# A fused low-rank projection: the pipeline re-made with hand-placed semaphores, bf16 pairs turned as fp32 words

## The chip, the cores and the metric

The kernel runs on one core of a Trainium2 chip. The core has a matrix engine (PE, with a separate row PEld for its weight loads), a vector engine (DVE), an activation engine (ACT), a general-purpose engine (GpSimd, called POOL in the profile), and SyncE (SP), which here only issues transfers. Sixteen DMA engines move data between the chip's memory (HBM) and the on-chip memory (SBUF, 128 partitions). PE writes its results to PSUM[...]. The metric is device time in microseconds (us), median of the runs; lower is better.

## What is computed

```python
x_flat = x.reshape(-1, in_dim)          # 32768 x 256, fp32
y = x_flat @ W                          # W 256 x 256
lora_out = x_flat @ lora_A              # rank 16
lora_out = lora_out * lora_E
lora_out = lora_out @ lora_B
y = y + scale * lora_out                # 32768 x 256, fp32
```

All factors on the right are small, so the kernel first builds one 256 x 256 matrix, W + scale * (lora_A * lora_E) @ lora_B, and then does one product with x. x and y are 33.55 MB each and have to be read and written once.

## The kernel before

The 32768 rows are cut into 8 chunks of 4096 rows (4 MB). In a chunk each of the 128 partitions holds 32 whole rows, so that a chunk's load or store is one contiguous run of 32 KB per partition. There are six chunk buffers in SBUF, called homes; a chunk's result is written over its own input, and the store leaves from there. A program that plans waits and semaphores by itself (the tile framework) decides the waits between engines; each engine works in the order of the code.

All transfers are issued by SyncE on one queue, in the order written in the list ORDER (lines 19 to 22): loads of chunks 0 to 5, then stores S0 and S1, load 6, store 2, load 7, stores 3 to 7. Chunk 0 is loaded in three pieces (8, 8 and 16 rows per partition), and the four small inputs are loaded after the first piece (lines 77 to 84). Loads 6 and 7 reuse the homes of chunks 0 and 1, so they wait until those stores have landed. A store waits until the whole chunk is computed.

The set-up (lines 89 to 108) makes an identity matrix on GpSimd, turns lora_A with PE, scales it on DVE, multiplies with lora_B on PE, and adds W on DVE into weff, in bf16.

The main loop (lines 110 to 133) handles a chunk in 16 groups of CG = 2 rows per partition, 256 rows. [...] x is turned first: four fp32 transposes of 128x128 into PSUM (psum_xt, line 118), a cast to bf16 by ACT from PSUM to SBUF (xt, line 123), four bf16 matmuls of 256 columns into psum_y (line 126), and a copy by DVE into the home (line 133). psum_xt and psum_y have three buffers each, xt has six. There are 128 such groups.

Of the kernel before, what the change touches and what calls it, by code (L numbers as in the profile page):

```python
# [1 line left out]

# [5 lines left out]

P = 128
FP32 = mybir.dt.float32  # L10
BF16 = mybir.dt.bfloat16


ROWS = 32
N_CHUNKS = 8
N_HOMES = 6
LOAD_PIECES = {0: [8, 8, 16]}

ORDER = [
    "L0", "L1", "L2", "L3", "L4", "L5",  # L20
    "S0", "S1", "L6", "S2", "L7", "S3", "S4", "S5", "S6", "S7",
]
CG = 2


@with_exitstack
def kernel(
    ctx: ExitStack,
    tc: tile.TileContext,
    x: bass.AP,  # L30
    W: bass.AP,
    lora_A: bass.AP,
    lora_B: bass.AP,
    lora_E: bass.AP,
    scale: bass.AP,
    out: bass.AP,
):
    nc = tc.nc
    x_flat = x.flatten_outer_dims()
    out_flat = out.flatten_outer_dims()  # L40
    N, K = x_flat.shape
    M = out_flat.shape[1]
    R = lora_B.shape[0]
    KC = K // P
    assert N == N_CHUNKS * ROWS * P and K == M

    const = ctx.enter_context(tc.tile_pool(name="const", bufs=1))
    homes_pool = ctx.enter_context(tc.tile_pool(name="homes", bufs=1))
    xTpool = ctx.enter_context(tc.tile_pool(name="xTpool", bufs=6))
    ps_setup = ctx.enter_context(tc.tile_pool(name="ps_setup", bufs=1, space=bass.MemoryType.PSUM))  # L50
    ps_xT = ctx.enter_context(tc.tile_pool(name="ps_xT", bufs=3, space=bass.MemoryType.PSUM))
    ps_y = ctx.enter_context(tc.tile_pool(name="ps_y", bufs=3, space=bass.MemoryType.PSUM))

    x_chunks = x_flat.rearrange("(c p b) k -> c p b k", p=P, b=ROWS)
    y_chunks = out_flat.rearrange("(c p b) m -> c p b m", p=P, b=ROWS)

    homes = [
        homes_pool.tile([P, ROWS, K], FP32, name=f"home{h}", tag=f"home{h}")
        for h in range(N_HOMES)
    ]  # L60

    def load(c, s, e):
        nc.sync.dma_start(out=homes[c % N_HOMES][:, s:e, :], in_=x_chunks[c, :, s:e, :])  # L63

    def store(c, s, e):
        nc.sync.dma_start(out=y_chunks[c, :, s:e, :], in_=homes[c % N_HOMES][:, s:e, :])

    def pieces(c):
        s = 0
        for n in LOAD_PIECES.get(c, [ROWS]):  # L70
            yield s, s + n
            s += n

    first = list(pieces(0))
    load(0, *first[0])

    w_sb = const.tile([P, KC, M], FP32)
    nc.sync.dma_start(out=w_sb, in_=W.rearrange("(c p) m -> p c m", p=P))  # L78
    a_sb = const.tile([P, KC, R], FP32)
    nc.sync.dma_start(out=a_sb, in_=lora_A.rearrange("(c p) r -> p c r", p=P))  # L80
    e_sb = const.tile([R, 1], FP32)
    nc.sync.dma_start(out=e_sb, in_=lora_E[:, None])
    b_sb = const.tile([R, M], FP32)
    nc.sync.dma_start(out=b_sb, in_=lora_B)

    for s, e in first[1:]:
        load(0, s, e)

    ident = const.tile([P, P], FP32)
    make_identity(nc, ident)  # L90

    ps_at = ps_setup.tile([R, KC, P], FP32, name="ps_at")
    for c in range(KC):
        nc.tensor.transpose(ps_at[:, c, :], a_sb[:, c, :], ident)  # L94
    ate = const.tile([R, KC, P], FP32)
    nc.vector.tensor_scalar(
        out=ate,
        in0=ps_at,
        scalar1=e_sb,
        scalar2=float(scale),  # L100
        op0=mybir.AluOpType.mult,
        op1=mybir.AluOpType.mult,
    )
    ps_aeb = ps_setup.tile([P, KC, M], FP32, name="ps_aeb")
    for c in range(KC):
        nc.tensor.matmul(ps_aeb[:, c, :], ate[:, c, :], b_sb, start=True, stop=True)  # L106
    weff = const.tile([P, KC, M], BF16)
    nc.vector.tensor_add(out=weff, in0=w_sb, in1=ps_aeb)

    def compute(c):  # L110
        home = homes[c % N_HOMES]
        for g in range(ROWS // CG):
            psum_xt = ps_xT.tile([P, CG, KC, P], FP32, name="psum_xt")
            xt = xTpool.tile([P, CG, KC, P], BF16, name="xt")
            psum_y = ps_y.tile([P, CG, M], FP32, name="psum_y")
            for j in range(CG):
                for k in range(KC):
                    nc.tensor.transpose(  # L118
                        psum_xt[:, j, k, :],
                        home[:, g * CG + j, k * P:(k + 1) * P],  # L120
                        ident,
                    )
            nc.scalar.copy(out=xt, in_=psum_xt)  # L123
            for j in range(CG):
                for k in range(KC):
                    nc.tensor.matmul(  # L126
                        psum_y[:, j, :],
                        xt[:, j, k, :],
                        weff[:, k, :],
                        start=(k == 0),  # L130
                        stop=(k == KC - 1),
                    )
            nc.vector.tensor_copy(out=home[:, g * CG:(g + 1) * CG, :], in_=psum_y)  # L133

    done = -1
    for step in ORDER:
        c = int(step[1:])
        if step[0] == "L":
            if c:
                for s, e in pieces(c):  # L140
                    load(c, s, e)
        else:
            while done < c:
                done += 1
                compute(done)
            store(c, 0, ROWS)


# [1 line left out]
_INS = ['x', 'W', 'lora_A', 'lora_B', 'lora_E', 'scale']  # L150
_OUTS = [((16, 2048, 256), 'float32')]

_NUMBERS = {'scale': 1.0}


# [26 lines left out]
```

## Time and profile before

| what | value |
|---|---|
| time, median of 3 runs | 165.19 us (165.09 to 165.42) |
| span of the profiled run | 163.4 us |
| PE busy | 131.9 us (81%) |
| PE weight loads busy | 101.6 us (62%) |
| DVE busy | 83.8 us (51%) |
| ACT busy | 70.3 us (43%) |
| GpSimd busy | 0.7 us |
| DMA | 67.56 MB, mean 414 GB/s |

The span is the time from the first to the last instruction of the profiled run; the device time is a little longer. An engine's busy share is an average over the whole span, and says nothing on whether another engine waits for it. The page cuts the span into 40 slices of about 4.1 us, with one digit of busy share (in tenths) for each engine and for the DMA engines, so one can see which row is full where. The group lines give, for one line of code, the operation, its shape, how often it ran, its mean duration and what it waited for:

```profile
L123 ACT CAST xt<-psum_xt 128x512 bf16<-128x512 f32 x128 | 69.0, 588 | 73.5 <-PE psum_xt L118 73.4
L126 PE MATMUL psum_y<-weff,xt 128*128 128x256 bf16 x512 | 71.9, 279 | 6.5 <-ACT xt L123 2.2
L133 DVE COPY home_73<-psum_y 128x512 f32<-128x512 f32 x32 | 20.8, 686 | 15.3 <-PE psum_y L126 15.3
```

The first line reads: ACT ran 128 casts of 512 elements per partition, 69.0 us in all, 588 ns each, and stood idle 73.5 us before them, nearly all of it until PE had finished a transpose.

### The profile page before, as it was taken

Reading aid. Unit: us, or ns where it says so; the run is one execution under the profiler, and the core shown is the slowest. Engines: PE = TensorE matmul, PEld = TensorE weight load, DVE = VectorE, ACT = ScalarE, POOL = GpSimd, SP = SyncE. Lnnn points to the kernel's source line nnn. Section 1 sums busy time; section 2 is a strip of 40 time slices with the busy share of each in tenths; the row PEclk is TensorE's granted clock in tenths of the full one; section 3 lists DMA queues with packets and bytes.
Section 4 is the critical chain, followed back from the end, with each engine's and each line's share of the span. In section 5 each row is a group of like instructions: output and inputs, shape, how many; then the busy total and the mean of one; then the engine's idle time right before and its main releaser. Section 6 shows DMA issues by size and latency. Waiting matters only on the chain.

```text
span 163.4 us, 2576 instructions
## 1 busy us (share of the span) xinstructions
PE 131.9 (81%) x1030; PEld 101.6 (62%) x1030; DVE 83.8 (51%) x130; ACT 70.3 (43%) x129; POOL 0.7 (0%) x6
## 2 busy tenths in 40 slices
PE   0399998999999999999999999998999899940000
PEld 0278775777777777777777777767777677730000
DVE  0115666466666666666666666665566556650000
ACT  3022555455555555555555555554555555520000
POOL 1000000000000000000000000000000000000000
PEclk9999999999999999999999999999999999997555
DMA  5999999998999998999999999999999999999991
GB/s 191 393 447 453 409 489 381 457 441 385 477 417 387 473 413 377 443 441 405 457 409 425 469 393 441 449 397 433 451 393 469 409 433 465 393 437 449 393 425 64
DMA packets 3211, 67.56 MB, mean 414 GB/s; under 512 B 624, under 2 KB 896, under 8 KB 896
## 3 DMA queue, kind: packets, MB, share of 16 engines
q1 hardware_dynamic: 3200, 67.41, 96.9%
q8 instruction: 8, 0.13, 0.3%
q14 instruction: 3, 0.02, 0.0%
HBM read 33.85 MB, written 33.55 MB: 413 GB/s over the span
## 4 chain that ended last, share of the span: by engine, by line
PE 58%; ACT 22%; issue 5%; DMA 3%; ACTq 1%; SPq 0%; DVEq 0%; DVE 0%
PE psum_y L126 43%; ACT xt L123 22%; PE psum_xt L118 13%; DMA a_sb<-in_lora_A_dram 3%; PE ps_aeb L106 1%; ACTq L123 1%; DVEq L177 0%; PE ps_at L94 0%; SPq L78 0%; SPq L63 0%; DVE home_74 L133 0%
## 5 line engine op out<-in xcount | busy, mean ns | idle before, releaser
L123 ACT CAST xt<-psum_xt 128x512 bf16<-128x512 f32 x128 | 69.0, 588 | 73.5 <-PE psum_xt L118 73.4
L126 PE MATMUL psum_y<-weff,xt 128*128 128x256 bf16 x512 | 71.9, 279 | 6.5 <-ACT xt L123 2.2
L126 PEld LDWEIGHTS <-xt 128*128 128x128 bf16 x512 | 40.5, 99 | 34.5 <-ACT xt L123 31.0
L133 DVE COPY home_73<-psum_y 128x512 f32<-128x512 f32 x32 | 20.8, 686 | 15.3 <-PE psum_y L126 15.3
L133 DVE COPY home_74<-psum_y 128x512 f32<-128x512 f32 x32 | 20.6, 686 | 13.0 <-PE psum_y L126 13.0
L118 PE MATMUL psum_xt<-ident,home_73 128*128 128x128 f32 x128 | 19.1, 295 | 0.0
L118 PEld LDWEIGHTS psum_xt<-ident,home_73 128*128 128x128 f32 x128 | 16.4, 154 | 1.0 <-issue 0.7
L118 PE MATMUL psum_xt<-ident,home_74 128*128 128x128 f32 x128 | 16.6, 273 | 0.0
L118 PEld LDWEIGHTS psum_xt<-ident,home_74 128*128 128x128 f32 x128 | 14.5, 141 | 0.2
L133 DVE COPY home_75<-psum_y 128x512 f32<-128x512 f32 x16 | 10.3, 686 | 6.1 <-PE psum_y L126 6.1
L133 DVE COPY home_76<-psum_y 128x512 f32<-128x512 f32 x16 | 10.3, 686 | 6.1 <-PE psum_y L126 6.1
L133 DVE COPY home_77<-psum_y 128x512 f32<-128x512 f32 x16 | 10.3, 686 | 6.1 <-PE psum_y L126 6.1
L133 DVE COPY home_78<-psum_y 128x512 f32<-128x512 f32 x16 | 10.3, 686 | 6.1 <-PE psum_y L126 6.1
L118 PE MATMUL psum_xt<-ident,home_75 128*128 128x128 f32 x64 | 8.5, 273 | 0.0
L118 PE MATMUL psum_xt<-ident,home_76 128*128 128x128 f32 x64 | 8.5, 273 | 0.0
L118 PE MATMUL psum_xt<-ident,home_77 128*128 128x128 f32 x64 | 8.5, 273 | 0.0
L118 PE MATMUL psum_xt<-ident,home_78 128*128 128x128 f32 x64 | 8.5, 273 | 0.0
L118 PEld LDWEIGHTS psum_xt<-ident,home_76 128*128 128x128 f32 x64 | 7.3, 141 | 0.1
L118 PEld LDWEIGHTS psum_xt<-ident,home_78 128*128 128x128 f32 x64 | 7.3, 141 | 0.1
L118 PEld LDWEIGHTS psum_xt<-ident,home_75 128*128 128x128 f32 x64 | 7.3, 141 | 0.1
L118 PEld LDWEIGHTS psum_xt<-ident,home_77 128*128 128x128 f32 x64 | 7.3, 141 | 0.1
L94 PE MATMUL ps_at<-ident,a_sb 128*16 128x128 f32 x2 | 0.6, 394 | 6.8 <-DMA a_sb<-in_lora_A_dram 6.8
(12 smaller groups left out, 6.7 us busy)
## 6 DMA issues: line engine op xcount, KB each, us to landing
home_74<-in_x_dram SPq DMA_DIRECT2D x2, 4096.0 KB, 24.4
out_dram<-home_73 SPq DMA_DIRECT2D x2, 4096.0 KB, 33.9
out_dram<-home_74 SPq DMA_DIRECT2D x2, 4096.0 KB, 26.8
home_75<-in_x_dram SPq DMA_DIRECT2D x1, 4096.0 KB, 29.1
home_76<-in_x_dram SPq DMA_DIRECT2D x1, 4096.0 KB, 38.0
home_77<-in_x_dram SPq DMA_DIRECT2D x1, 4096.0 KB, 47.4
home_78<-in_x_dram SPq DMA_DIRECT2D x1, 4096.0 KB, 57.4
home_73<-in_x_dram SPq DMA_DIRECT2D x1, 4096.0 KB, 19.3
```

Source lines behind the costliest of these rows:

```text
L94: nc.tensor.transpose(ps_at[:, c, :], a_sb[:, c, :], ident)
L106: nc.tensor.matmul(ps_aeb[:, c, :], ate[:, c, :], b_sb, start=True, stop=True)
L118: nc.tensor.transpose(psum_xt[:, j, k, :], home[:, g * CG + j, k * P:(k + 1) * P], ident,)
L123: nc.scalar.copy(out=xt, in_=psum_xt)
L126: nc.tensor.matmul(psum_y[:, j, :], xt[:, j, k, :], weff[:, k, :], start=(k == 0), stop=(k == KC - 1),)
L133: nc.vector.tensor_copy(out=home[:, g * CG:(g + 1) * CG, :], in_=psum_y)
```

## The change

The planned waits are replaced by hand-placed semaphores in one block (a critical block in the framework's words), in which each engine has its own program. The computation of a group changes too:

- A group has CG = 4 rows per partition, 512 rows; there are 64 groups.
- GpSimd first casts the fp32 rows to bf16 into a staging buffer (stage, two buffers).
- PE turns the staged rows as fp32 words: one word holds a pair of neighbouring bf16 values, so one row of 256 values is 128 words and needs one 128x128 transpose in place of two. There are 256 transposes in place of 512.
- ACT copies the turned words from PSUM to SBUF and takes the even and odd halves apart (psum_xt read as bf16 with a step of two), since after the turn partition q holds the inputs 2q and 2q+1. The matrix weff is laid out to match: W and lora_A are loaded with "(q t) m -> q t m", which is one contiguous run per partition.
- The 8 matmuls of a group, 512 in all, are as before; DVE copies 1024 elements per partition at once.
- PE's program is a hardware loop of 10 rounds with 6 groups each, and 4 groups after it; it takes semaphores by waiting for 1 and counting down. The other engines' programs are written out.
- Buffers are fixed: two stage, two xt, two psum_xt and three psum_y[...].

Its purpose is to take work off PE and off the planner's synchronisation. SyncE's order of transfers, the six homes and the three first pieces stay. The core of the diff:

```diff
-CG = 2
+CG = 4
+GPC = ROWS // CG
+N_GROUPS = N_CHUNKS * GPC
+NS, NX, NT, NY = 2, 2, 2, 3
...
+    stage = [sbuf(f"stage{i}", [P, CG, K], BF16) for i in range(NS)]
+    xt = [sbuf(f"xt{i}", [P, CG, KT, P], BF16) for i in range(NX)]
...
+    with tc.tile_critical(no_gpsimd_drain=True):
+        with nc.Block(no_gpsimd_drain=True) as block:
+            @block.sync
+            def _(sync):
...
+                    if c >= N_HOMES:
+                        sync.wait_ge(stored_of[c - N_HOMES], 16)
+                    sync.dma_start(out=home[:, s:e, :], in_=x_chunks[c, :, s:e, :]).then_inc(loaded[pc], 16)
...
+                        sync.wait_ge(s_chunk, c + 1)
+                        sync.dma_start(out=y_chunks[c], in_=homes[c % N_HOMES][:]).then_inc(
+                            stored_of.get(c, stored_rest), 16
+                        )
+                sync.wait_ge(stored_rest, 16 * (N_CHUNKS - len(stored_of)))
...
+            @block.gpsimd
...
+                    if g >= NS:
+                        gpsimd.wait_ge(s_turned, g - NS + 1)
+                    gpsimd.tensor_copy(
+                        out=stage[g % NS][:], in_=homes[c % N_HOMES][:, b:b + CG, :]
+                    ).then_inc(s_stage, 1)
...
+                def turn(i):
+                    take(s_stage)
+                    words = stage[i % NS][:].bitcast(FP32)
+                    for b in range(CG):
+                        ins = tensor.transpose(psum_xt[i % NT][:, b, :], words[:, b, :], ident[:])
+                    ins.then_inc(s_turned, 1)
+                def multiply(i):
+                    take(s_xt)
+                    take(s_free)
...
+                with tensor.Fori(0, (N_GROUPS - 4) // unroll):
+                    for i in range(unroll):
+                        turn(i + 1)
+                        multiply(i)
...
+            @block.scalar
...
+                    scalar.wait_ge(s_turned, g + 1)
+                    if g >= NX:
+                        scalar.wait_ge(s_y, g - NX + 1)
+                    halves = psum_xt[g % NT][:].bitcast(BF16).rearrange("q b (p t) -> q b t p", t=KT)
+                    scalar.copy(out=xt[g % NX][:], in_=halves).then_inc(s_xt, 1)
...
+                    vector.wait_ge(s_y, g + 1)
+                    vector.tensor_copy(
+                        out=homes[c % N_HOMES][:, b:b + CG, :], in_=psum_y[g % NY][:]
+                    ).then_inc(s_free, 1)
+                    if g % GPC == GPC - 1:
+                        vector.drain().then_inc(s_chunk, 1)
+        nc.clear_and_free_semaphores(nc.allocated_since(before))
```

## The prediction

> **What bounds the kernel now.** I read the slices over time first, because they show whether one resource is full from end to end.
>
> ```profile
> PE   0399998999999999999999999998999899940000
> ACT  3022555455555555555555555554555555520000
> POOL 1000000000000000000000000000000000000000
> DMA  5999999998999998999999999999999999999991
> q1 hardware_dynamic: 3200, 67.41, 96.9%
> ```
>
> Two rows are full: PE and DMA. PE is full for 36 of 40 slices, then idle for the last 15 us. DMA is full from the first slice to the last, and its queue was moving data for 96.9% of the span. The load and the store of 33.55 MB each can't be avoided, so I asked at what rate the queue moves them, and whether that rate follows the compute engines. Busy time by stage (columns: stretch, its length, then the engines' busy time, granted clock, DMA share and GB/s):
>
> ```profile
> 0.00:2.00 2.00, 0.00 (x0) 0.00 (x0) 0.00 (x0) 1.26 (x1) 0.70 (x6) 1.00 0.23 37
> 2.00:4.00 2.00, 0.00 (x0) 0.00 (x0) 0.00 (x0) 0.02 (x1) 0.00 (x0) 1.00 0.89 344
> 4.00:10.00 6.00, 3.16 (x10) 1.94 (x10) 0.47 (x1) 0.00 (x0) 0.00 (x0) 1.00 1.03 406
> 10.00:57.00 47.00, 44.90 (x344) 35.30 (x343) 27.90 (x43) 23.31 (x43) 0.00 (x0) 1.00 1.01 435
> 57.00:110.00 53.00, 50.99 (x415) 39.38 (x414) 33.20 (x53) 27.62 (x53) 0.00 (x0) 1.00 1.00 426
> 110.00:150.00 40.00, 32.84 (x266) 24.98 (x264) 22.25 (x35) 18.09 (x34) 0.00 (x0) 0.99 1.00 430
> 150.00:158.00 8.00, 0.00 (x0) 0.00 (x0) 0.00 (x0) 0.00 (x0) 0.00 (x0) 0.50 1.01 438
> 158.00:160.00 2.00, 0.00 (x0) 0.00 (x0) 0.00 (x0) 0.00 (x0) 0.00 (x0) 0.50 0.61 262
> 160.00:161.00 1.00, 0.00 (x0) 0.00 (x0) 0.00 (x0) 0.00 (x0) 0.00 (x0) 0.50 0.23 98
> ```
>
> From 10 to 158 us the rate stays at 426 to 438 GB/s: loads alone, mixed traffic, stores, and the last 8 us with every engine idle. So the compute engines don't slow the DMA, and a faster engine can't speed it up.
>
> The remaining question is whether the DMA ever ran out of work because a store was issued late. The wait list of the SyncE queue and the issue times answer it:
>
> ```profile
> SPq L63 <- DMA out_dram<-home_73: 27.3, 1, 27.3
> SPq L66 <- DVE home_78 L133: 16.0, 1, 16.0
> 146.11 0.33 SPq L66 DMA_DIRECT2D out_dram<-home_74  x1
> DMA to landing us min/median/max: 16.3/33.8/44.3
> ```
>
> SyncE does wait up to 16 us for DVE before a store, but the last store, issued at 146.11, still took 16.3 us to land. A chunk of 4.19 MB at 430 GB/s takes 9.75 us. Allowing some 1.5 to 2 us for stragglers and the completion signal, about 4.5 us of older work lay in front of it. All earlier stores took longer to land, so they too queued behind work. Compute finishes early enough with some 4.5 us to spare. The chain of waits shows 43% on PE at L126 and 22% on ACT at L123, but it follows compute to 146 us, not the full queue.
>
> [...]
>
> **The change part by part.**
>
> *PE.* The chain repeats one 2.05 us cycle (matmuls start at 38.73 and 40.78), with 8 matmuls in 1.10 us, so 8 transposes get the other 0.95. A new 4-row group has the same 8 matmuls but 4 transposes, since one fp32 word carries two bf16: 1.10 + 0.48 = 1.58 us. Over 64 groups that is 101 us against 131.
>
> *ACT.* 512 elements took 588 ns. [...] The strided half-word read is not in the trace[...]. I take 1.0, ends 1.0 and 1.9.
>
> *DVE.* [...] 1.22 us for 1024, 78 us in all.
>
> *Pool, new.* 64 casts of 128x1024, fp32 to bf16. Nearest rows: the memset of 128x128 took 204 ns against 98 to 101 for one column, 0.8 ns an element; the affine select 292 ns, so about 1.5 ns an element above a fixed 100. That brackets a cast at 0.94 to 1.64 us[...]. I take 1.6[...].
>
> *Do these hide?* Compute may end as late as 145.5 + 4.5 = 150 us; the first cast can start at about 6.3 us (first piece issued at 0.74, landing after 5.3). With some 3 us through the pipeline, a group may take (150 - 9.3)/64 = 2.2 us. All four engines sit at or below 1.6. Hence the whole compute change lies under the full DMA queue, and is worth nothing in itself. The last chunk would be ready near 130 us (its load lands at 84.2 + about 29.5 = 113.7, then 8 x 1.6 and 3 us), and its store waits 16 us longer in the queue.
>
> *The new waits.* On PE, behind the wait for a cast stand the matmuls of the previous group; behind the wait for a free PSUM buffer stand the next transposes. On ACT, the wait on y for buffer reuse holds the cast that PE wants next. Two stage, two xt and three y buffers with a 1.58 us PE period leave each of the others (1.0 to 1.6) time, and the same 2.2 us allowance covers slips. The loop jumps 10 times; to eat the 39 us between 101 and 140, each jump would have to cost 3.9 us. SyncE's order and its two waits for landed stores are unchanged.
>
> *What isn't hidden: the ends.* Before the first load, SyncE now passes an entry signal of the critical block and two more branches[...]. With a semaphore hop I take +0.2 us, ends 0.1 and 0.5. After the last landing comes one more all-engine barrier, a semaphore clear and an exit signal. The trace has SyncE waiting 0.6 us for two closing barriers, so 0.3 each; +0.45, ends 0.2 and 1.0. W and lora_A now load in contiguous rows per partition, 256 packets fewer. The stretch from 4 to 10 us moved 406 GB/s instead of 432, so all small packets cost (26/432) x 6 = 0.36 us; half would be 0.18, I take -0.1. Sum: +0.55.
>
> Forecast: 165.19 + 0.55 = 165.74, say 165.7 us.
>
> **The rivals.**
> *A better DMA start or finish, faster.* Until 4 us the DMA lost 2 x (430-37)/430 + 2 x (430-344)/430 = 2.2 us, and from 158 to 161 us stragglers cost 2 x (430-262)/430 + (430-98)/430 = 1.55 us. A far smaller program fetches fewer instructions (0.15 MB on the two instruction queues before), and these fetches sit on the same 16 engines. If a third of the straggling and the packets went, that is -0.6: 164.6. Against it: the ramp is set by SyncE's issues, which stay, and instruction queues took only 0.3%.
> *Pool becomes the bound, slower.* [...] For it: Pool has nothing else that shows its price for a cast. Against: both nearest rows give at most 1.64.
> *Waits or loop jumps stretch a group slightly past 2.2 us.* At 2.25 the end moves by 64 x 0.05 = 3 us: 168.7. For it: few buffers; against: 0.6 us of slack per group.
>
> **How the numbers follow.** Forecast (slightly slower) 0.66, better start or finish 0.22, Pool 0.07, stretched groups 0.05. Within the forecast the ends give 165.3 to 166.6; the 0.2% line is at 165.52, so three quarters of it, 0.5, counts as slower. With the last two rivals that is 0.60; same 0.19; faster 0.21. The range leaves out the Pool case and the best of the faster case: 164.7 to 167.4.
>
> **What would show it.** Right: DMA again near 430 GB/s from 10 to 158 us, PE busy far less, the last store issued near 130 us and landing after some 32 us, the span longer by half a microsecond at its ends. A Pool cast above 2.2 us, or a gap in the DMA slices after 110 us, would mean a compute bound; a DMA rate above 440 GB/s would overturn the whole reasoning.

## The result and the profile after

The changed kernel took 166.47 us (166.16 to 166.83, 4 runs) against 165.31 us (165.09 to 165.49, 4 runs) of the kernel before on the same chip: ratio 1.0072, 95% interval 1.0046 to 1.0098. Run once more beside other kernels, it took 165.85 us (165.73 to 166.07, 5 runs) against 165.24: ratio 1.0044, interval 1.0031 to 1.0057. It is slower, by 0.6 us in one measurement and 1.2 us in the other; the forecast was 0.55.

The slices over time of the changed kernel, the rows that answer to those of before:

```profile
PE   0399949999999999999910099900999300000000
ACT  3043734576777777676710047610476000000000
POOL 1453627577777777777400267303673000000000
PEclk9999996999999999999995569995699955555555
DMA  5999998989989998999999999999999999999960
q1 hardware_dynamic: 2944, 67.41, 96.2%
```

PE now stands idle for whole slices (from about 86 us and 106 us on, until the next chunk has landed) and ends 16 us earlier. DMA is full as before; the queue moves the same 67.41 MB in 256 packets fewer. The group lines of the new operations:

```profile
L230 DVE COPY home<-psum_y 128x1024 f32<-128x1024 f32 x64 | 78.4, 1225 | 41.1 <-PE psum_y L172 38.2
L150 POOL CAST stage<-home 128x1024 bf16<-128x1024 f32 x64 | 66.4, 1043 | 57.0 <-DMA home<-in_x_dram 33.2
L210 ACT COPY xt<-psum_xt 128x1024 bf16<-128x1024 bf16 x64 | 64.8, 1012 | 60.9 <-PE psum_xt L164 60.9
L164 PE MATMUL psum_xt<-ident,stage 128*128 128x128 f32 x256 | 41.6, 288 | 21.9 <-PEq L157 21.9
```

GpSimd's main wait is now for loads: compute has caught up with the transfers. Next, the stretches of the changed kernel, in the columns of the table shown for the kernel before:

```profile
0.00:2.00 2.00, 0.00 (x0) 0.00 (x0) 0.00 (x0) 1.10 (x1) 0.70 (x6) 1.00 0.12 20
2.00:4.00 2.00, 0.00 (x0) 0.00 (x0) 0.00 (x0) 0.19 (x1) 0.00 (x0) 1.00 0.90 307
4.00:10.00 6.00, 3.31 (x10) 2.14 (x10) 0.47 (x1) 1.01 (x1) 2.97 (x3) 1.00 1.04 423
10.00:57.00 47.00, 44.25 (x347) 36.82 (x347) 34.75 (x29) 28.90 (x29) 29.70 (x30) 0.96 1.02 437
57.00:110.00 53.00, 38.25 (x317) 31.83 (x314) 33.30 (x28) 26.77 (x27) 25.48 (x25) 0.90 1.00 424
110.00:150.00 40.00, 13.59 (x104) 11.21 (x104) 11.02 (x9) 8.10 (x8) 8.29 (x8) 0.68 1.00 432
158.00:160.00 2.00, 0.00 (x0) 0.00 (x0) 0.00 (x0) 0.00 (x0) 0.00 (x0) 0.50 0.65 279
160.00:161.00 1.00, 0.00 (x0) 0.00 (x0) 0.00 (x0) 0.00 (x0) 0.00 (x0) 0.50 0.00 0
161.00:162.00 1.00, 0.00 (x0) 0.00 (x0) 0.00 (x0) 0.00 (x0) 0.00 (x0) 0.50 0.08 33
```

From 10 to 150 us the rates are those of before. Three stretches differ: less in the first 4 us (20 and 307 GB/s against 37 and 344), more from 4 to 10 us (423 against 406), and a last packet of some 33 KB (33 GB/s for 1 us) that starts after 161 us. (The view counts a packet where it starts; one of 32 KB takes 1.21 us.) Last, SyncE's queue: its closing waits and the last store's issue and landing.

```profile
0.95 0.38 SPq L106 DMA_DIRECT2D home<-in_x_dram  x1
130.51 0.33 SPq L125 DMA_DIRECT2D out_dram<-home  x1
DMA to landing us min/median/max: 32.4/32.4/32.4
SPq L97 <- DMA out_dram<-home: 32.0, 1, 32.0
SPq L97 <- PEq L97: 0.2, 1, 0.2
```

The first load is issued at 0.95 us, not 0.74: +0.2. The last store is issued 15.6 us earlier than before and waits as much longer: it lands at 162.9 us, where the one of before landed at 162.4. From that landing to the end of the span are 1.6 us (164.5), before 1.0 (163.4): +0.6, with one barrier more (line 97, 0.2 us). So of the span's 1.1 us more, 0.2 lie ahead of the first load, 0.6 behind the last landing, and 0.3 somewhere in the transfers.

### The profile page after: what moved, and what is told of

Read it like the earlier page. It is cut to its first block, busy times and chain, and to the rows that moved or that the text cites. A ratio compares the mean times of both kernels' runs of the same rounds, so it can differ in the third digit from the quotient of the medians.

```text
span 164.5 us, 2139 instructions
## 1 busy us (share of the span) xinstructions
PE 99.4 (60%) x774; PEld 82.0 (50%) x774; DVE 79.5 (48%) x66; ACT 66.1 (40%) x65; POOL 67.1 (41%) x70
## 3 DMA queue, kind: packets, MB, share of 16 engines
q1 hardware_dynamic: 2944, 67.41, 96.2%
## 5 line engine op out<-in xcount | busy, mean ns | idle before, releaser
L230 DVE COPY home<-psum_y 128x1024 f32<-128x1024 f32 x64 | 78.4, 1225 | 41.1 <-PE psum_y L172 38.2
L150 POOL CAST stage<-home 128x1024 bf16<-128x1024 f32 x64 | 66.4, 1043 | 57.0 <-DMA home<-in_x_dram 33.2
L210 ACT COPY xt<-psum_xt 128x1024 bf16<-128x1024 bf16 x64 | 64.8, 1012 | 60.9 <-PE psum_xt L164 60.9
L172 PE MATMUL psum_y<-weff,xt 128*128 128x256 bf16 x512 | 71.0, 284 | 1.2 <-PEq L157 0.5
L172 PEld LDWEIGHTS psum_y<-weff,xt 128*128 128x128 bf16 x512 | 48.4, 101 | 15.3 <-issue 7.3
L164 PE MATMUL psum_xt<-ident,stage 128*128 128x128 f32 x256 | 41.6, 288 | 21.9 <-PEq L157 21.9
L164 PEld LDWEIGHTS psum_xt<-ident,stage 128*128 128x128 f32 x256 | 32.5, 151 | 24.4 <-issue 23.3
L190 PE MATMUL psum_y<-b_sb,ate 16*128 16x256 f32 x4 | 2.1, 670 | 0.0
L226 DVE TENSOR_TENSOR weff<-w_sb,psum_y 128x512 bf16<-128x512 f32 x1 | 0.7, 686 | 2.4 <-PE psum_y L190 2.4
L190 PEld LDWEIGHTS psum_y<-b_sb,ate 16*128 16x128 f32 x4 | 1.2, 319 | 0.5 <-issue 0.3
```

The source lines that it names most:

```text
L150: gpsimd.tensor_copy(out=stage[g % NS][:], in_=homes[c % N_HOMES][:, b:b + CG, :]).then_inc(s_stage, 1)
L164: ins = tensor.transpose(psum_xt[i % NT][:, b, :], words[:, b, :], ident[:])
L172: ins = tensor.matmul(psum_y[i % NY][:, b, :], xt[i % NX][:, b, t, :], weff[:, t, :], start=(t == 0), stop=(t == KT - 1),)
L190: ins = tensor.matmul(psum_y[1][:, t, :], ate[:, t, :], b_sb[:], start=True, stop=True)
L210: scalar.copy(out=xt[g % NX][:], in_=halves).then_inc(s_xt, 1)
L226: vector.tensor_add(out=weff[:], in0=w_sb[:], in1=psum_y[1][:, :KT, :]).then_inc(s_free, NY)
```

## The experiments

My theory: only the frame around the work (entry, closing barrier, clearing of semaphores) costs time, about 0.8 us, and the new computation neither helps nor harms. Rivals: the new computation harms the transfers, through GpSimd's traffic or through stores piled up early in the queue; or the closing isn't on the path. In the table, "landing" is the issue of the last store plus its time to landing, "tail" the rest of the span. Times are medians; the other columns are those of the one profiled execution, so a row need not add up.

| kernel | time us | first load | landing | tail |
|---|---|---|---|---|
| before | 165.2 to 165.3 | 0.74 | 162.4 | 1.0 |
| changed | 166.47 | 0.95 | 162.9 | 1.6 |
| changed, again | 165.85 | 0.95 | 162.3 | 1.6 |
| before, no groups | 162.64 | 0.74 | 159.6 | 1.0 |
| changed, no groups | 163.43 | 0.95 | 160.4 | 1.6 |
| new computation, old frame | 165.11 | 0.74 | 162.5 | 1.0 |
| changed, wait moved out of the block | 165.53 | 0.95 | 162.6 | 1.2 |

**The transfers alone, in both frames.** The groups are left out, so what was loaded is stored.

```diff
 # kernel before
             while done < c:
                 done += 1
-                compute(done)
+                pass
 # changed kernel: no casts, no PE, ACT and DVE loops; DVE signals a chunk when it is loaded
+                for c in range(N_CHUNKS):
+                    for pc in pieces:
+                        if pc[0] == c:
+                            vector.wait_ge(loaded[pc], 16)
+                    vector.drain().then_inc(s_chunk, 1)
```

> The kernel before without its 128 groups (no turning, no products, no copies: what was loaded is stored, so the output is x); all loads, stores and the set-up of the weights stay. If the transfers alone set the time, 165.2 us within 0.3, the last store landing near 162.4 us. If engines at work in the on-chip memory slowed the transfers, clearly less, 164.5 or below. If a deep backlog of stores hurts (here every store is issued as soon as its load lands), about 0.3 more, 165.6.

> The changed kernel without its 64 groups (output is x again); block, semaphores, order of transfers and set-up stay. If the frame (entry, closing barrier, clearing of semaphores) costs what the change lost, 166.1 to 166.5 us, 0.8 above the same cut of the kernel before: first load issued 0.2 us later, 0.6 us more between the last landing and the end. If the new compute (GpSimd's casts beside the transfers) is the cost, 165.3.

Measured: 162.64 us (162.3 to 162.68; 0.9838 of before, interval 0.9824 to 0.9852) and 163.43 us (163.35 to 163.75; 0.9884, 0.9868 to 0.9901). The difference between the frames is 0.79 us, as expected. But both are some 2.6 us or more faster than I expected: work on the engines does cost transfer time. I had ruled that out from the even rates. The end of the kernel before without groups shows how (same columns without ACT):

```profile
110.00:150.00 40.00, 0.00 (x0) 0.00 (x0) 0.00 (x0) 0.00 (x0) 1.00 1.00 433
150.00:158.00 8.00, 0.00 (x0) 0.00 (x0) 0.00 (x0) 0.00 (x0) 1.00 1.05 455
158.00:160.00 2.00, 0.00 (x0) 0.00 (x0) 0.00 (x0) 0.00 (x0) 1.00 0.04 16
```

Only one packet of 32 KB starts after 158 us (16 GB/s for 2 us), and the last store landed at 159.6 us. In the kernel before, packets for 262 GB/s started in the same two microseconds and for 98 GB/s in the third. What I had called stragglers goes away with the groups: the mean rate hardly moves (433 against 430 GB/s from 110 to 150 us), since a lag of few engines is thin in a mean over 16, but the last one sets the end.

**Stores paced as before.** Each cast is done twice, the first into a buffer that nobody reads, so a group takes longer.

```diff
+                    gpsimd.tensor_copy(out=waste[:], in_=homes[c % N_HOMES][:, b:b + CG, :]).then_inc(s_waste, 1)
+                    gpsimd.wait_ge(s_waste, g + 1)
                     gpsimd.tensor_copy(
                         out=stage[g % NS][:], in_=homes[c % N_HOMES][:, b:b + CG, :]
```

> The changed kernel with each cast on GpSimd done twice, once into a buffer nobody reads: about 2.15 us a group, so that the last store is issued near 147 us as in the kernel before, not at 130.5. If only the frame costs, no change: 166.4 us. If the early stores (a longer backlog in the queue) spread the DMA engines' ends, 0.3 less, 166.1. If the pace of compute mattered at all, more: 64 x 0.6 = 38 us at the most.

Measured: 165.93 us (165.48 to 166.9), between the two measurements of the changed kernel. The last store was issued at 145.0 us and landed 17.4 us later, at 162.4. GpSimd's busy time nearly doubled (130.6 us against 67.1), and neither that nor the later stores moved the time beyond the spread of the changed kernel. So compute has slack, and the early stores are not shown to cost or give anything.

**The closing.** SyncE's wait for the last stores moves out of the block, to GpSimd behind the closing barrier.

```diff
-                sync.wait_ge(stored_rest, 16 * (N_CHUNKS - len(stored_of)))
...
+        nc.gpsimd.wait_ge(stored_rest, 16 * (N_CHUNKS - len(stored_of)))
         nc.clear_and_free_semaphores(nc.allocated_since(before))
```

> The changed kernel with the wait for the last stores moved from SyncE inside the block to GpSimd behind the block's closing barrier, so that this barrier lies under the transfers and only the clearing of the semaphores and the outer barriers come after the last landing. If the closing costs 0.6 us more than before, some 0.3 us of it goes: 166.1 to 166.2 us, 1.3 us from landing to end. If the end is not on the path, 166.5.

Measured: 165.53 us (165.09 to 166.46, 22 runs), ratio to before 1.0021, interval 1.0009 to 1.0033. Its tail is 1.2 us, not 1.6: the barrier of the block is on the path, and hiding it gives 0.4. Against the second measurement of the changed kernel (165.85) the time fell by 0.3, as expected; against the first by 0.9, more than the tail can explain.

**The computation and the frame apart.** The changed kernel again, and its computation written in the frame of the kernel before.

```diff
 # kernel before, with
-CG = 2
+CG = 4
...
+            nc.gpsimd.tensor_copy(out=stage, in_=home[:, g * CG:(g + 1) * CG, :])
+            words = stage[:].bitcast(FP32)
             for j in range(CG):
-                for k in range(KC):
-                    nc.tensor.transpose(psum_xt[:, j, k, :], home[...], ident)
-            nc.scalar.copy(out=xt, in_=psum_xt)
+                nc.tensor.transpose(psum_xt[:, j, :], words[:, j, :], ident)
+            halves = psum_xt[:].bitcast(BF16).rearrange("q b (p t) -> q b t p", t=KC)
+            nc.scalar.copy(out=xt, in_=halves)
```

> The changed kernel once more, beside the next three on one chip: 166.4 us. Its last landing shows how far the last DMA engine trails from one execution to the next; if that tail is chance, it lies anywhere between 161.9 and 162.9 us.

> The new computation (casts on GpSimd, bf16 pairs turned as fp32 words, groups of 512 rows, contiguous weight loads) in the frame of the kernel before: planned waits, no block, no loop. If the frame costs 0.8 us and the computation nothing, 0.8 below the changed kernel: 165.5 us, first load issued at 0.74, 1.0 us from landing to end. If the new computation is what costs, as slow as the changed kernel: 166.4.

Measured: 165.85 us, and 165.11 us (164.65 to 165.55, 13 runs; ratio to before 0.9996, interval 0.9985 to 1.0007). The frame costs 0.74 us here, 0.79 without groups. The new computation alone makes no measurable difference, although it takes 34.6 us of busy time off PE (97.3 against 131.9). This settles the main question: of what the changed kernel lost, these 0.7 us are the frame's.

The second profile of the changed kernel ends so:

```profile
158.00:160.00 2.00, 0.00 (x0) 0.00 (x0) 0.00 (x0) 0.00 (x0) 0.00 (x0) 0.50 0.57 246
160.00:161.00 1.00, 0.00 (x0) 0.00 (x0) 0.00 (x0) 0.00 (x0) 0.00 (x0) 0.50 0.08 33
161.00:162.00 1.00, 0.00 (x0) 0.00 (x0) 0.00 (x0) 0.00 (x0) 0.00 (x0) 0.50 0.00 0
```

One packet starts after 160 us, none after 161: the last engine trailed less than in the first profile, and the landing is 0.6 us earlier (162.3 against 162.9). Head and tail are the same in both. That is as large as the difference of the two measured times; why the trailing differs between them is not known.

**What makes a DMA engine trail.** Five kernels, all the changed kernel without its groups (163.43 us), with work that nobody waits for. (In the runs with copies and with the long reduce SyncE waits for the loads itself, since DVE is busy.)

```diff
 # PE only
+                tensor.wait_ge(s_free, NY)
+                with tensor.Fori(0, 40):
+                    for i in range(24):
+                        tensor.matmul(psum_y[2][:, 0, :], weff[:, 0, :P], weff[:, 0, :], start=True, stop=True)
 # copies only, with the like on ACT (100 casts) and on DVE (170 copies from psum_y)
+                for i in range(100):
+                    gpsimd.tensor_copy(out=waste_p[:], in_=homes[2][:, :CG, :]).then_inc(s_p, 1)
 # tiny matmuls: Fori(0, 90), and in the last run Fori(0, 230)
+                        tensor.matmul(psum_y[2][:1, 0, :1], weff[:1, 0, :1], weff[:1, 0, :1], start=True, stop=True)
 # long reduce
+                for i in range(12):
+                    vector.tensor_reduce(out=waste_d[:], in_=homes[2][:], axis=mybir.AxisListType.X, op=ALU.max)
```

> The changed kernel without its groups, but with 960 matmuls of 256 columns on PE from one fixed tile, from 11 to about 140 us, that nobody waits for (output is x). Without them it took 163.4. If PE's activity is what slows one DMA engine during the stores, 165 to 165.7 with one engine ending 1 to 2 us after the others; if not, 163.4.

> The changed kernel without its groups, but with GpSimd casting, ACT copying and DVE copying from PSUM on scratch buffers, each on its own, from about 30 to 145 us (output is x). If the copies' traffic in the on-chip memory slows one DMA engine, 165 to 165.7; if not, 163.4.

> The changed kernel without its groups, but with 2160 matmuls of a single element on PE from 11 us on, that nobody waits for (output is x): many instructions, next to no traffic. If the number of instructions executed during the stores is what holds one DMA engine back, one engine ends 1 to 2.5 us after the rest and the time is 165 to 166; if traffic or load of the engines is, 163.4.

> The changed kernel without its groups, but with DVE reading a whole 4 MB home 12 times, 12 instructions of some 9 us, from 30 to about 140 us (output is x): much traffic, hardly any instructions. If traffic holds one DMA engine back, 165 to 166; if the number of instructions does, 163.4 with all DMA engines ending within 0.6 us.

> As the run with tiny matmuls, but 5520 of them, so that PE issues them until about 157 us and not only until 68 us, over the whole stretch of the stores (output is x). If the number of instructions executed while stores are under way holds one DMA engine back, 165 us or more and one engine ending late; if the engines' traffic or load does, 163.5 again.

Measured: PE alone 164.95 us (164.51 to 165.96), the copies alone 165.65 (165.6 to 166.03), each with a packet still moving after 160 us; 12 long reduces 163.26 (163.2 to 163.59), no loss. 2160 tiny matmuls 163.64 (163.46 to 163.88), but they were over by 68 us, when the stores had only begun, so this run could not decide. The run with 5520 of them, active until about 149 us, does: 176.02 us (175.9 to 176.25). Its page and the end of its stretches:

```profile
PE   0279999999999999999999999999999999200000
DMA  5999999899998989998999989999899998994000
```

```profile
110.00:150.00 40.00, 39.24 (x1570) 39.13 (x1566) 0.00 (x0) 0.00 (x0) 1.00 1.00 428
158.00:160.00 2.00, 0.00 (x0) 0.00 (x0) 0.00 (x0) 0.00 (x0) 1.00 0.38 164
162.00:165.00 3.00, 0.00 (x0) 0.00 (x0) 0.00 (x0) 0.00 (x0) 1.00 0.08 33
168.00:174.00 6.00, 0.00 (x0) 0.00 (x0) 0.00 (x0) 0.00 (x0) 1.00 0.04 16
```

After 160 us the share is 0.08, about one engine of 16, and packets still start until about 171 us: one DMA engine had fallen that far behind, while the rate of all from 110 to 150 us still reads 428 GB/s. These matmuls of one element move next to no data, and the long reduces read 4 MB each with no loss. So, in this frame and with matmuls, what holds one engine back goes with the number of instructions executed during the stores, not with their traffic. From 60 to 150 us this run executed 2006 + 2003 + 1570 + 1566 = 7145 matmuls and weight loads, and its span is 12.2 us longer than without (174.2 against 162.0): 1.7 ns each. PE alone executed 1071 in the same stretch for 1.5 us more span (163.5 against 162.0), 1.4 ns each. The copies alone do not fit this count: 370 instructions went with 1.7 us more (163.7), 4.6 ns each. What in an instruction does it stays open. One rival is untested: every execution here was recorded by the profiler, with an entry for each instruction. If writing these entries held the engine back, the runs would look the same; only times without recording could tell.

**Where the lag arises.** Each transfer raises its semaphore 16 times in the trace, which I take as once by each DMA engine. The time from the first to the last of the 16, in us, shows how far the last engine lags (the transfers stand in the order in which they landed in the traces; in the kernel before, load 4 landed at 54.3 us, load 5 at 64.7 and the first store at 74.4):

| transfer | before | new computation, old frame | before, no groups | changed | 5520 matmuls |
|---|---|---|---|---|---|
| load 1 | 0.49 | 0.62 | 0.53 | 0.34 | 0.40 |
| load 4 | 1.89 | 1.90 | 0.53 | 0.34 | 0.39 |
| load 5 | 2.34 | 2.85 | 0.31 | 1.11 | 0.50 |
| store 1 | 2.17 | 2.86 | 0.26 | 1.09 | 4.52 |
| load 6 | 2.29 | 2.80 | 0.46 | 1.67 | 4.73 |
| store 2 | 2.20 | 2.76 | 0.44 | 1.91 | 6.84 |
| store 7 | 3.11 | 3.44 | 0.52 | 3.43 | 13.28 |

In the block, the lag grows after load 4; with 5520 matmuls by some 2 us in each of stores 1 and 2, and by 0.2 in load 6 between them, at the same pace of matmuls. With the planned waits, more than half of it is there at load 4 (1.89 of 3.11 us in the kernel before), 20 us before the first store landed. The old frame has more of a second kind of traffic, the fetching of instructions (here of the kernel before, the new computation in the old frame, and the changed kernel, in this order; the kernels without groups have no such row):

```profile
q8 instruction: 8, 0.13, 0.3%
q8 instruction: 6, 0.10, 0.2%
q8 instruction: 1, 0.02, 0.0%
```

A data packet of 32 KB takes 1.21 us. Between 14 and 58 us of the kernel before only three took clearly longer, 1.59 to 1.69 us, and each started as an instruction fetch ended (fetches of 1.1, 1.1 and 0.3 us at 25.5, 43.8 and 49.7 us). So a fetch of 16 KB puts 1.3 us on one engine: the lag goes from 0.49 to 1.77 at load 2. In the stores the kernel before shows the other kind too: from 64 to 143 us, packets that follow one another as on one engine take about 1.28 us (48 of them), in the run with 5520 matmuls 1.51. In the kernel before three engines landed last, at 162.1 to 162.4 us, and the others by 161.0, so freeing one of them would have gained little. That fetches are the cause in the old frame is read from the trace; no run leaves out the fetches alone. The copies' lag comes in steps, 0.65 us at load 4 (behind a fetch at 43.5 us), 0.65 at load 5 and 1.2 at load 6, and does not grow from store 3 to store 7 (2.68 and 2.67). The last two steps stay open.

## Why the prediction was right, and where it was off

*Direction and bound: right.* A full DMA queue hides the compute change. Shown by the new computation in the old frame (no difference) and by the doubled cast (no difference beyond the spread). The 4.5 us to spare rested on an allowance of 1.5 to 2 us, which was my estimate; the doubled cast's last store, issued at 145.0 us, landed 17.4 us later at the same 162.4 us as in the kernel before.

*Engine costs: right, but for GpSimd, which was cheaper.* DVE 1.22 forecast, 1.225 measured; ACT 1.0 forecast, 1.012 measured. Both forecasts were my estimates: in the trace of before, the groups' copies and casts have 512 elements only. From 512 to 1024 elements the mean grew by 424 ns on ACT (588 to 1012) and by 539 on DVE (686 to 1225). The strided half-word read shows no price of its own: on ACT a plain cast of 1024 elements from SBUF took 1045 ns in the run with the copies alone. GpSimd 1.6 forecast, 1.043 measured, 1.02 ns an element, near the lower end of the 0.94 to 1.64 us read from its memset and its affine select. The first two stores were issued 12.2 us apart, 1.53 us a group, against 1.58 forecast. The last store was forecast near 130 us with a landing after some 32, and came at 130.5 with 32.4.

*Head: right* (+0.2 forecast, my estimate, not shown in the trace of before; 0.21 measured). *Tail: too small* (+0.45 forecast, 0.6 measured; the upper end was 1.0). *Packets: too small.* From 4 to 10 us, 423 against 406 GB/s is (423-406)/430 x 6 = 0.24 us gained, where I took 0.1. Head, tail and packets with these sizes give +0.57, against 0.55.

*What the forecast did not have.* In the first measurement the time rose by 1.16 us. Beyond the frame's 0.74 to 0.79, the trailing engine made up the rest: its landing came 0.5 us later than before, though only 0.2 of that was the later start. In the second, it did not, and the rise was 0.61.

*The step that failed* is "the compute engines don't slow the DMA, and a faster engine can't speed it up". Leaving the groups out gave 2.6 us. It did no harm to the forecast only because the new computation loses about as much in the block as the old one did before: 165.85 - 163.43 = 2.4 us, 165.2 - 162.6 = 2.6 us. That was luck, since the two losses arise in different places: before, most of it is there by the end of the loads; in the block it comes with the stores. The faster rival had one of the causes right: it named the stragglers and the fetching of instructions on the same 16 engines. The fetches did fall, from 11 packets to 4, and with them the lag in the loads (at load 4 from 1.89 to 0.34 us); but an engine held back in the stores took the place of the ones held back by fetches, so the end came no earlier.

*The slower rivals* (GpSimd or stretched groups as the bound; that a cast might take longer than 1.64 us was my estimate) fell with the 1.04 us cast. One sum is off: the chances of slower (0.50, 0.07 and 0.05) add up to 0.62, not 0.60.

## What to carry to other kernels

Where the DMA queue is full from end to end and the last store still waits in it for a long time, work saved on an engine shows up only as idle time (here 34.6 us of PE's busy time, for 165.11 us against 165.2): first ask how much of the last transfer's time to landing is queueing. Then only the ends count, and a hand-made block with its own entry, closing barrier and semaphore clearing costs there (0.75 us in this case), and less with its last wait put behind the barrier (1.2 us from landing to end, not 1.6). And look at the last microseconds of the DMA rate: one trailing engine out of 16 doesn't show in a mean, but sets the end (with 5520 matmuls 428 GB/s from 110 to 150 us, and 176.02 us). Then compare the 16 landing signals of each transfer: they tell in which stretch the engine fell behind, before one looks for a cause.

## What the runs showed of the hardware that I had not expected

- A fetch of 16 KB of instructions took 0.9 to 1.1 us (8 of them in the kernel before), and the data packet behind it ran up to 0.5 us longer (1.69 us against 1.21). With the first of them the last engine's lag went from 0.49 to 1.77 us (load 2), and it stayed at 1.77 us or more to the end.
- Executing instructions while stores are under way went with one DMA engine falling behind: 5520 matmuls of one element put 12.2 us on the span, at next to no data. Whether the instructions or their recording do it is open. Traffic in SBUF alone did not do it: 12 reduces that each read 4 MB there cost nothing (span 161.8 us against 162.0). Yet with its groups left out the kernel before ended 2.6 us sooner.
- At the change from loads to stores the rate dipped with and without the engines at work: from 57 to 64 us 391 GB/s before, 380 changed, 393 in the block without groups, against 431 to 433 from 64 to 110 us. Without groups in the old frame it was 417.
- PE's granted clock falls in and just after the pauses (tenths of 5 to 6 in the slices from 86 to 99 us), and this cost nothing here: the last store was issued at 130.5 us and then took 32.4 us to land.
